# Two-layer hybrid decoder trunk: first unit of each layer and of an output projection as eight half products, forms ahead of the weights' splits

## The chip, the cores and the metric

The kernel runs on one core of a Trainium2 chip. The metric is the device time of one execution in microseconds (us), given as the median of several runs. Engines are called by their short names: PE is TensorE (matrix products, transposes), DVE is VectorE, ACT is ScalarE, POOL is GpSimd, SP is SyncE (it starts most transfers).

## The reference

Two layers work on x of 512 tokens and 2048 channels, one sequence. Cut to what matters:

```python
def fox_branch(x, w_in, b_f, q_gain, k_gain, w_out):        # layer 1, 16 heads of 128
    q, k, v, gate, f_logit = split(x @ w_in)                # 2048 -> 4 * 2048 + 16
    q, k = rms_norm(heads(q), q_gain), rms_norm(heads(k), k_gain)
    c = cumsum(log_sigmoid(f_logit + b_f))                  # the forget gate, per head
    p = softmax(causal(q @ k.T * scale + c[:, None] - c[None, :]))
    return (p @ v * silu(gate)) @ w_out                     # 2048 -> 2048

def retention_branch(x, w_in, w_out):                       # layer 2, 8 heads, qk 256, v 512
    q, k, v, gate = split(x @ w_in)                         # 2048 -> 2 * 2048 + 2 * 4096
    o = retain(rotary(q), rotary(k), v)                     # chunks of 128 with decay
    return (group_norm_heads(o) * silu(gate)) @ w_out       # 4096 -> 2048

x = layer_norm(alpha * x + fox_branch(x, ...))
x = layer_norm(alpha * x + retention_branch(x, ...))
```

Everything is float32.

## The kernel before

**Products.** Each factor of a large product is split into a high and a low part (`split`, L251 to L256): ACT rounds it into `h` (L255), then DVE subtracts to get `l` (L256). `mm3` (L258 to L262) makes high x high, high x low and low x high, three matmuls for one product.

**Units.** The projections are cut into 34 units. A unit takes the 512 tokens by 2048 input channels of one activation times a piece of the weights: narrow units 512 output columns (16 of them: q and k of a pair of heads), wide ones 1024 (18: gate and value, and the output projections). A `Unit` is computed by a scheme with seven products of quarters. The activation is cut into a11, a12, a21, a22: first index the half of the tokens, second the half of the input channels. The products use *forms* of it (`FORM`, L38): p1 a11, p2 a12, p3 s4, p4 a22, p5 s1, p6 s2, p7 s3, where s1 = a21 - a22, s2 = s1 - a11, s4 = s2 + a12, s3 = a11 - a21 (signs as the kernel keeps them). Weight quarters are summed likewise on DVE (L447, L451) and then split. Each product is worked in *blocks*: 2 blocks of 24 matmuls with 256 columns in a narrow unit, 4 blocks of 12 matmuls with 512 columns in a wide one. Results gather in three banks of accumulators (b0 to b2), are kept in SBUF by ACT (L339), combined on DVE (L367, L372, L377) and given to a *sink*, which is what the unit is for: `Pair.take` (q, k), `gate_and_value`, `add_z` (residual sum and statistics for the layer norm).

**Forms.** A form is made once and used by many units. x's quarters come from memory (`form_of_x`, `quarter_of_x`), and `combine` (L530) makes s1, s2, s4, s3 and a22 from them, a sum and a split at a time. For an output projection the heads write their output, with signs, into DRAM tiles that add up to the forms (`give_forms`, L588), and `fetch_form` (L596) loads and splits them (`y_raw`). The last two heads of layer 1 skip DRAM: `last_heads` (L923) splits their part of every form from the head's own output. Between the layers `to_columns` (L1109) normalises, transposes on PE (L1162) and evicts with the norm's gain (L1150 on DVE, L1152 on ACT), from which forms are made again.

**The order.** It is fixed when the program is built, by the class `Order`. Each block is a slot. In `slot` (L158) the weights are loaded up to 9 blocks ahead, summed and split 2 to 3 blocks ahead (`split_one`), the block is multiplied, then other work (heads, sinks, forms) takes one step per task (`step`, L114), as long as the estimated queues of DVE and ACT stay below 5.0. Before a block is multiplied, `require(b.ready)` (L134) lets such steps go until its form is there; by then the weights of the next blocks have been split already.

**The sequence.** Layer 1: `begin` (L510) with the first q/k unit and the first gate/value unit, on a11 and a12 (p1, p2), then the REST of both; then units in turn, with heads spawned by `core`. A pair's q and k are squared and summed on ACT (L756), scaled, transposed (L780), split (L774, L775), and each head's scores, softmax and values follow (`head`, L785). Two wide units make the output projection: unit 4 in the order `HELD`, unit 5 in `EARLY`. Layer 2 starts with `begin` again, then heads 1 to 7, then units 14 to 17, of which the last is `EARLY` too and ends in `store` (L1423): norm factors on DVE, two DVE steps for 512 columns (L1432, L1433), transfers to the output.

```python
BEGIN = (("p1",), ("p2",))
HELD = ([("p1", c) for c in range(4)] + [(p, c) for p in ("p5", "p6", "p2") for c in range(3)]
        + [(p, 3) for p in ("p5", "p6")] + blocks_of(4, ("p3", "p7")) + [("p2", 3)] + blocks_of(4, ("p4",)))
EARLY = (("p1", "p5"), ("p2", "p6"), ("p3",), ("p7",), ("p4",))
```

Of the kernel before, what the change touches and what calls it, by code (L numbers as in the profile page):

```python
# [17 lines left out]
P = 128  # L18
D = 2048
S = 512  # L20
# [19 lines left out]
        "s3": ("f10", "f11"), "a22": ("f12", "f13")}  # L40
# [3 lines left out]
def blocks_of(n, *groups):  # L44
# [4 lines left out]
BEGIN = (("p1",), ("p2",))  # L49
# [3 lines left out]
EARLY = (("p1", "p5"), ("p2", "p6"), ("p3",), ("p7",), ("p4",))  # L53

HELD = ([("p1", c) for c in range(4)] + [(p, c) for p in ("p5", "p6", "p2") for c in range(3)]
        + [(p, 3) for p in ("p5", "p6")] + blocks_of(4, ("p3", "p7")) + [("p2", 3)] + blocks_of(4, ("p4",)))
# [8 lines left out]
RINGS = dict(mmp=2, tmp=4, st=3, q=4, **{t: 1 for t in "k0 k1 k2 in0 in1 g0 g1 g2 d0 b0 b1 b2".split()})  # L65

# [9 lines left out]
class Order:  # L76
# [29 lines left out]
    def spawn(self, steps, front=False):  # L106
        task = dict(steps=steps, last=self.now - 1)
        try:
            task["need"] = next(steps)
        except StopIteration:  # L110
            return
        self.tasks.insert(0, task) if front else self.tasks.append(task)

    def step(self, forced=False):  # L114
        for task in list(self.tasks):
            n = task["need"]
            if self.now < task["last"] + n.get("wait", 1) or not n.get("until", lambda: True)():
                continue
# [3 lines left out]
            if not forced and any(d + c > 5.0 and c for d, c in zip(self.debt, cost)):  # L122
                continue
            self.debt = [d + c for d, c in zip(self.debt, cost)]
            self.time += n.get("pe", 0)
            task["last"] = self.now
            try:
                task["need"] = next(task["steps"])
            except StopIteration:
                self.tasks.remove(task)  # L130

    time = 0.0

    def require(self, met):  # L134
        for _ in range(400):
            if met():
                return
            self.turn()
            self.debt = [max(0.0, d - 2.7) for d in self.debt]
            self.step(True)  # L140
# [44 lines left out]
    def split_one(self):  # L185
        self.line[self.split].split()
        self.split += 1
        self.debt[0] += 1.22
        self.debt[1] += 1.06
# [7 lines left out]
def trunk(ctx: ExitStack, tc: tile.TileContext, xq, x, fb_f, columns, wf_in, narrow, wide, ln_g, ln_b, rot, decay,  # L197
# [80 lines left out]
    class Unit:  # L278
# [3 lines left out]
        def __init__(self, w, n, sink, rows=True, u2="k0"):  # L282
# [4 lines left out]
            self.tags = self.both = None  # L287
            self.early = False
            self.bank, self.kept, self.chain, self.lent, self.summed = {}, {}, {}, {}, {}
            self.left = {p: self.blocks for p in FORM}  # L290

# [3 lines left out]
        def accumulator(self, b):  # L295
            if self.both is None:
                if self.tags is None:
                    self.tags = dict(zip("xzy", banks))
                    banks[:] = banks[1:] + banks[:1]
                require(lambda: free[self.tags[b]])  # L300
                take(self.tags[b])
                t = psum.tile([P, 2, 512], F32, name="acc", tag=self.tags[b])
                return t if self.wide else t[:, 0].rearrange("p (e n) -> p e n", e=2)
            if b == "z":
                require(lambda: free[self.third])
                take(self.third)
                t = psum.tile([P, 2, 512], F32, name="acc", tag=self.third)[:, 0]
            else:
                if b == "x":
                    require(lambda: free[self.both])  # L310
                    take(self.both)
                    self.pair = psum.tile([P, 2, 512], F32, name="acc", tag=self.both)
                t = self.pair[:, int(b == "y")]
            return t.rearrange("p (e n) -> p e n", e=2)

        def leave(self, b):

            if self.both is None:
                give(self.tags[b])
            elif b != "y":  # L320
                give({"x": self.both, "z": self.third}[b])
# [32 lines left out]
        def after(self, p):  # L354
# [21 lines left out]
            if p == "p7":  # L376
                nc.vector.tensor_sub(k["p5"][0], k["p5"][0], b["x"])  # L377
                o.debt[0] += cost
                self.hand(1, 1, "p5")
            if p == "p4" and not self.early:  # L380
                self.sink(1, 0, b["x"], lambda after=0: self.leave("x"))
            if p == "p4" and self.early:
# [1111 lines left out]
```

## Time and profile before

| | |
|---|---|
| median of 3 runs | 2819.68 us (2817.28 to 2823.34) |
| the profiled execution: its time | 2814.23 us |
| its span in the trace | 2812.5 us |
| granted PE clock, mean | 0.931 of full |
| instructions | 34239 |
| moved by DMA | 488.98 MB, 174 GB/s |

The span is the time from the first to the last record of the profiled execution; all times inside it are counted from its start. Busy times of engines overlap. PEclk is the clock that PE was granted, as a share of full speed. In the rows of a timeline stand start, duration, engine, line, operation, output <- inputs, shape, and in brackets how long the engine had been idle before and what it then got.

### The profile page before, as it was taken

To read this page: it belongs to the slowest core of one execution; us is meant where nothing else is said; L and a number is where in the kernel's file an instruction comes from. 1 tells how busy PE (TensorE), PEld (TensorE's weight loads), DVE (VectorE), ACT (ScalarE), POOL (GpSimd) and SP (SyncE) were. 2 spreads that over 40 slices of the span, in tenths; PEclk is the share of its full clock that TensorE was granted. 3 is DMA by queue.
4 is the path that set the end of the run, shared out by engine and by line. 5 is a ranking of instruction groups with operands and counts; after the bars stand their busy time and mean duration, and the time that the engine had idled before them with its cause. 6 is when DMAs were issued, how large, how long until landed. Compare 5 with 4: busy or idle time off the path is not lost. (4 is left out here: it accounts for less than half of the span.)

```text
span 2812.5 us, 34239 instructions
## 1 busy us (share of the span) xinstructions
PE 2421.5 (86%) x12820; PEld 2044.4 (73%) x12820; DVE 2015.2 (72%) x2584; ACT 1280.6 (46%) x1898; POOL 190.8 (7%) x284
## 2 busy tenths in 40 slices
PE   6589989989997668875899999999999999699965
PEld 5478778788787447654687979797979787577754
DVE  5467767767766437754687888888888888677858
ACT  4244655655655533352344454545444445444422
POOL 0000100100100100100001010101010000010000
PEclk9699999999998679986999999999999999899987
DMA  5344654644645327632456575756575757587773
GB/s 204 105 151 145 184 164 147 199 149 143 187 150 172 103 86 230 210 127 69 145 186 191 180 211 168 201 161 195 176 213 170 212 159 235 149 252 245 228 230 118
DMA packets 195638, 488.98 MB, mean 174 GB/s; under 512 B 19264, under 2 KB 70080, under 8 KB 195216
## 3 DMA queue, kind: packets, MB, share of 16 engines
q1 hardware_dynamic: 165904, 415.74, 44.5%
q0 software_dynamic: 29568, 71.06, 11.0%
q8 instruction: 101, 1.65, 0.2%
q14 instruction: 65, 0.53, 0.1%
HBM read 419.84 MB, written 66.88 MB: 173 GB/s over the span
## 5 line engine op out<-in xcount | busy, mean ns | idle before, releaser
L255 ACT ACTIVATE w_h<-w_q 128x1024 fp32r<-128x1024 f32 x408 | 429.9, 1058 | 770.4 <-DVE w_q L451 531.9
L256 DVE TENSOR_TENSOR w_l<-w_q,w_h 128x1024 fp32r<-128x1024 f32 x408 | 497.9, 1223 | 334.7 <-ACT w_h L255 331.5
L260 PE MATMUL acc<-w_h,s 128*128 128x512 f32 (+1 forms) x1664 | 619.9, 373 | 98.3 <-ACT s L255 60.8
L261 PE MATMUL acc<-w_l,s 128*128 128x512 f32 (+1 forms) x1664 | 618.2, 372 | 34.2 <-DVE w_l L256 34.0
L262 PE MATMUL acc<-w_h,s 128*128 128x512 f32 (+1 forms) x1664 | 609.7, 366 | 9.5 <-DVE s L256 9.4
L256 DVE TENSOR_TENSOR w_l<-w_raw,w_h 128x1024 fp32r<-128x1024 f32 x312 | 380.3, 1223 | 255.0 <-ACT w_h L255 253.1
L260 PE MATMUL acc<-w_h,a 128*128 128x512 f32 (+1 forms) x1248 | 466.8, 374 | 63.4 <-ACT w_h L255 21.2
L255 ACT ACTIVATE w_h<-w_raw 128x1024 fp32r<-128x1024 f32 x312 | 326.3, 1054 | 372.2 <-DVE w_raw L447 192.9
L262 PE MATMUL acc<-w_h,a 128*128 128x512 f32 (+1 forms) x1248 | 459.9, 369 | 5.0 <-DVE a L256 5.0
L261 PE MATMUL acc<-w_l,a 128*128 128x512 f32 (+1 forms) x1248 | 460.2, 369 | 2.3 <-DVE w_l L256 2.3
L260 PEld LDWEIGHTS acc<-w_h,s 128*128 128x128 f32 x1664 | 326.3, 196 | 159.2 <-ACT s L255 65.3
L261 PEld LDWEIGHTS acc<-w_l,s 128*128 128x128 f32 x1664 | 325.9, 196 | 106.6 <-DVE w_l L256 63.5
L451 DVE TENSOR_TENSOR w_q<-w_q,w_raw 128x1024 f32<-128x1024 f32 x304 | 371.2, 1221 | 26.1 <-DMA w_raw<-in_wide 23.1
L262 PEld LDWEIGHTS acc<-w_h,s 128*128 128x128 f32 x1664 | 325.0, 195 | 58.4 <-DVE s L256 14.2
L260 PEld LDWEIGHTS acc<-w_h,a 128*128 128x128 f32 x1248 | 247.0, 198 | 103.8 <-issue 25.4
L262 PEld LDWEIGHTS acc<-w_h,a 128*128 128x128 f32 x1248 | 246.1, 197 | 44.7 <-DVE a L256 8.3
L261 PEld LDWEIGHTS acc<-w_l,a 128*128 128x128 f32 x1248 | 247.1, 198 | 38.4 <-DVE w_l L256 4.3
L260 PE MATMUL acc<-s,w_h 128*128 128x256 f32 x512 | 151.2, 295 | 31.5 <-ACT s L255 31.5
L261 PE MATMUL acc<-s,w_h 128*128 128x256 f32 x512 | 151.4, 296 | 7.4 <-DVE s L256 7.4
L262 PE MATMUL acc<-s,w_l 128*128 128x256 f32 x512 | 150.0, 293 | 0.0
L447 DVE TENSOR_TENSOR w_raw<-w_raw 128x1024 f32<-128x1024 f32 x96 | 117.0, 1219 | 23.9 <-DMA w_raw<-in_wide 23.9
L260 PEld LDWEIGHTS acc<-s,w_h 128*128 128x128 f32 x512 | 103.8, 203 | 34.2 <-ACT s L255 33.0
(206 smaller groups left out, 2956.2 us busy)
## 6 DMA issues: line engine op xcount, KB each, us to landing
w_raw<-in_wide SPq DMA_DIRECT2D x372, 512.0 KB, 3.6
w_raw<-in_narrow SPq DMA_DIRECT2D x164, 512.0 KB, 3.4
w_q<-in_wide SPq DMA_DIRECT2D x72, 512.0 KB, 4.2
w_q<-in_narrow SPq DMA_DIRECT2D x32, 512.0 KB, 4.4
y_s<-ny POOLq DMA_DIRECT2D x48, 256.0 KB, 6.9
y_s<-y POOLq DMA_DIRECT2D x40, 256.0 KB, 4.9
y_raw<-y_s SPq DMA_DIRECT2D x35, 256.0 KB, 4.9
y_raw<-y_a SPq DMA_DIRECT2D x26, 256.0 KB, 5.1
```

What stands on the lines that cost most here:

```text
L255: nc.scalar.activation(h, src, AF.Copy)
L256: nc.vector.tensor_sub(l, src, f32(h))
L260: nc.tensor.matmul(ps, a[0], b[0], start=start, stop=False, skip_group_check=True)
L261: nc.tensor.matmul(ps, a[0], b[1], start=False, stop=False, skip_group_check=True)
L262: nc.tensor.matmul(ps, a[1], b[0], start=False, stop=stop, skip_group_check=True)
L447: nc.vector.tensor_add(self.t, self.t, u.lent.pop(("p3", c)))
L451: nc.vector.tensor_add(u.chain[c], u.chain[c], t)
```

## The change

1. **Eight half products.** The first q/k unit of layer 1, the first q/k unit of layer 2 and the first unit of layer 1's output projection become units of a new class `Plain`. It computes C11 = a11 B1 + a12 B2 and so on directly: for both halves m of the tokens, both halves n of the output columns and both halves k of the input, the block (k, n, c, m) multiplies a form a(m)(k) by a weight block as it is. No weights are summed, a split weight block serves m = 0 and m = 1, and only the forms a11, a12, a21, a22 are used (a21 is a new form, at s3's place in SBUF). The orders are `BOTH` (layer 1), `EACH` (layer 2: first m = 0, then two products of the gate/value unit, then m = 1) and a new `HELD`. `begin`, `last_heads` and their parts go; heads 14 and 15 split only their a12 and a22.
2. **Order.** `split_one` first lets the form that a block needs go ahead of that block's weights' split. Tasks have ranks: sinks 0, forms and norms 1, heads 2; `step` goes on until no task goes any further. Limits are 4.8 (DVE) and 4.0 (ACT). A head's steps are cut finer.
3. **Smaller parts.** The squares for the norm of q and k are made by the sink, in place on the finished accumulator (L860 after), and `rsqrt` works in place; one more step stands between transposes and scores. `EARLY` makes p1, then p5; p7 and p4 are added to the residual in two parts, and the very last product in two halves. `store` works on one block of 128 tokens at a time, and half of the output transfers start on POOL's queue.

```diff
+BOTH = [(k, n, c, m) for k in (1, 2) for c in range(2) for n in range(2) for m in range(2)]
+EACH = [[(k, n, c, m) for k in (1, 2) for c in range(2) for n in range(2)] for m in range(2)]
-HELD = ([("p1", c) for c in range(4)] + [(p, c) for p in ("p5", "p6", "p2") for c in range(3)]
-        + [(p, 3) for p in ("p5", "p6")] + blocks_of(4, ("p3", "p7")) + [("p2", 3)] + blocks_of(4, ("p4",)))
+HELD = ([(1, 0, c, m) for c in range(4) for m in range(2)] + [(1, 1, c, 0) for c in range(4)]
+        + [(2, 0, c, m) for c in range(4) for m in range(2)] + [(1, 1, c, 1) for c in range(4)]
+        + [(2, 1, c, m) for c in range(4) for m in range(2)])
...
+    def step(self, forced=False, rank=2):
+
+        went = False
+        while self.each(forced, rank):
+            went = True
+        return went
...
     def split_one(self):
-        self.line[self.split].split()
+        b = self.line[self.split]
+        if b.before:
+            b.before()
+
+        self.require(b.ready)
+        if b.split():
+            self.debt[0] += 1.22
+            self.debt[1] += 1.06
         self.split += 1
-        self.debt[0] += 1.22
-        self.debt[1] += 1.06
...
+    class PlainBlock:
...
+        def split(self):
+            if self.same:
+                self.w = self.same.w
+                return False
+            self.w = [pool.tile(self.u.shape, F32R, name=f"w_{j}", tag=f"w_{j}", bufs=3) for j in "hl"]
+            split(self.t, *self.w)
+            give("st")
+            return True
+
+        def ready(self):
+            n = self.u.shape[1]
+            return ready.get(f"a{self.m + 1}{self.k}", set()).issuperset(range(n * self.c, n * self.c + n))
...
-            for s in range(ST):
-                yield need(act=2.0, mmp=1)
-                sq = by4(mmp())
-                for h in range(4):
-                    nc.scalar.activation(sq[:, h], raw[s][:, h * P:(h + 1) * P], AF.Square,
-                                         accum_out=ss[:, s, h:h + 1])
-                give("mmp")
...
-                yield from last_heads(head - 8, y)
-                give("tmp")
-                return
+
+                yield need(dve=0.8, act=0.8, until=lambda: len(ready["a12"]) >= 6 and len(ready["a22"]) >= 6)
+                for m in range(2):
+                    split_form(f"a{m + 1}2", y[:, None, m * 256:(m + 1) * 256], head - 8, head - 7)
...
-    Unit(wide, 4, sink).run(HELD, then={"p6": lambda s=steps: spawn(s())})
+    Plain(wide, 4, sink, last_banks).run(
+        HELD, then={8: lambda s=steps: spawn(s(), 1), 20: fetch("s1", "s2", "s4", "s3")})
...
-    begin(heads[0].qk_unit, heads[0].vg_unit, True)
-    for h in heads:
-        order = ORDER if h.h else REST
-        h.qk_unit.run(order, then={"p3": lambda h=h: spawn(h.attend())})
+    first.qk_unit.run(EACH[0], then={0: lambda: spawn(combine(True, first.qk_unit), 1)})
+    first.vg_unit.run(FIRST)
+    first.qk_unit.run(EACH[1], then={len(EACH[1]) - 1: lambda: spawn(first.attend())})
+    first.vg_unit.run(REST, then={"p4": lambda: spawn(first.retain())})
```

How this moves instructions is shown at three places. First DVE in the first two units, from the point where x's forms are split. Names are output <- inputs; `w_l` is the low part of a weight block, made from a loaded `w_raw` or a summed `w_q`; L545 is the sum for s1. Before:

```order
L256 TENSOR_TENSOR a12_176<-raw_145,a12_175 128x1024 x2
L256 TENSOR_TENSOR w_l_184<-w_raw_164,w_h_183 128x1024
L256 TENSOR_TENSOR w_l_217<-w_raw_173,w_h_216 128x1024
L256 TENSOR_TENSOR w_l_250<-w_raw_187,w_h_249 128x1024
L256 TENSOR_TENSOR w_l_281<-w_raw_189,w_h_280 128x1024
L367 TENSOR_TENSOR p15_246<-acc_191,p15_246 128x512
L256 TENSOR_TENSOR w_l_313<-w_raw_220,w_h_312 128x1024
L256 TENSOR_TENSOR w_l_336<-w_raw_253,w_h_335 128x1024
L256 TENSOR_TENSOR w_l_354<-w_raw_284,w_h_353 128x1024
```

And now the start of DVE's program:

```order
L282 TENSOR_TENSOR a11_153<-raw_143,a11_152 128x512 x2
L282 TENSOR_TENSOR w_l_159<-w_raw_149,w_h_158 128x1024
L282 TENSOR_TENSOR a21_165<-raw_145,a21_164 128x1024
L282 TENSOR_TENSOR w_l_169<-w_raw_162,w_h_168 128x1024
L282 TENSOR_TENSOR a11_153<-raw_143,a11_152 128x1024
L282 TENSOR_TENSOR w_l_236<-w_raw_173,w_h_235 128x1024
L282 TENSOR_TENSOR a21_165<-raw_145,a21_164 128x1024
L282 TENSOR_TENSOR w_l_292<-w_raw_176,w_h_291 128x1024
L282 TENSOR_TENSOR a12_348<-raw_144,a12_347 128x1024
L282 TENSOR_TENSOR w_l_352<-w_raw_179,w_h_351 128x1024
L282 TENSOR_TENSOR a22_382<-raw_146,a22_381 128x1024
L664 TENSOR_TENSOR raw_206<-raw_145,raw_146 128x1024
```

One form piece now stands ahead of each weight split, and the first sum for s1 (L664, L545 before) is the 12th row of the program instead of the 18th.

Second, ACT at the last two heads of layer 1: `o` is a head's output, `y_raw` a piece of a form loaded from DRAM, `y_s` a sum made in `last_heads`, `w_h` the high part of a weight block. Before, for the two heads:

```order
L255 ACTIVATE a12_7729<-y_raw_8409 128x512
L255 ACTIVATE w_h_8438<-w_raw_8352 128x1024
L255 ACTIVATE s4_7630<-y_raw_8453 128x512
L255 ACTIVATE a22_7806<-y_raw_8457 128x512
L255 ACTIVATE a12_7729<-o_8314 128x256
L255 ACTIVATE a22_7806<-o_8314 128x256
L255 ACTIVATE s1_7938<-y_s_8451 128x256
L255 ACTIVATE s2_7497<-y_s_8451 128x256
L255 ACTIVATE s4_7630<-y_s_8451 128x256
L897 ACTIVATE o_8474<-mmp_8445 128x512
L255 ACTIVATE a12_7729<-o_8474 128x256
```

Now:

```order
L281 ACTIVATE a12_7739<-o_8360 128x256
L281 ACTIVATE a22_7836<-o_8360 128x256
L922 ACTIVATE pT_8368<-mmp_8372 128x3x128
L1020 ACTIVATE ny_8389<-o_8360 128x512
L922 ACTIVATE pT_8368<-mmp_8383 128x2x128
L922 ACTIVATE pT_8368<-mmp_8383 128x128
L1004 ACTIVATE o_8402<-mmp_8397 128x512
L281 ACTIVATE a12_7739<-o_8402 128x256
L281 ACTIVATE a22_7836<-o_8402 128x256
L281 ACTIVATE w_h_8414<-w_raw_8005 128x1024
```

The s forms of these heads have gone from here, the loaded pieces stand further ahead, and the weights' split comes behind the forms.

Third, DVE where the second half of the tokens comes out of the layer norm's transposes at the start of layer 2 (`raw` is evicted, L1150 before, L1229 now). Before:

```order
L1150 TENSOR_SCALAR raw_9711<-mmp_9831,cols_75 128x128
L1150 TENSOR_SCALAR raw_9711<-mmp_9848,cols_75 128x128
L1150 TENSOR_SCALAR raw_9710<-mmp_9857,cols_75 128x128
L1150 TENSOR_SCALAR raw_9710<-mmp_9866,cols_75 128x128
L1150 TENSOR_SCALAR raw_9711<-mmp_9875,cols_75 128x128
L1150 TENSOR_SCALAR raw_9711<-mmp_9884,cols_75 128x128
L545 TENSOR_TENSOR raw_9896<-raw_9710,raw_9711 128x1024
L256 TENSOR_TENSOR s1_9898<-raw_9896,s1_9897 128x1024
```

Now:

```order
L1229 TENSOR_SCALAR raw_9688<-mmp_9744,cols_75 128x128
L282 TENSOR_TENSOR a21_9775<-raw_9688,a21_9774 128x1024
L282 TENSOR_TENSOR w_l_9779<-w_raw_9602,w_h_9778 128x1024
L1229 TENSOR_SCALAR raw_9689<-mmp_9769,cols_75 128x128
L282 TENSOR_TENSOR w_l_9806<-w_raw_9632,w_h_9805 128x1024
L1229 TENSOR_SCALAR raw_9689<-mmp_9800,cols_75 128x128
L282 TENSOR_TENSOR w_l_9835<-w_raw_9662,w_h_9834 128x1024
L1229 TENSOR_SCALAR raw_9688<-mmp_9827,cols_75 128x128
```

The evictions stand one by one between the weights' splits of blocks that use a11 and a12, and a21 is split as soon as its half is there; s1's sum stands 15 rows below the last one shown.

591 lines of the change are left out of this document (322 added, 269 removed).

## The prediction

> **What bounds the kernel now.** The page came first: its busy line and two rows of its table of slices, which share the span into 40 (digits are tenths).
>
> ```profile
> PE 2421.5 (86%) x12820; PEld 2044.4 (73%) x12820; DVE 2015.2 (72%) x2584; ACT 1280.6 (46%) x1898; POOL 190.8 (7%) x284
> ...
> PE   6589989989997668875899999999999999699965
> ...
> PEclk9699999999998679986999999999999999899987
> ```
>
> TensorE is the bound wherever its digit is 9, so only the dips can give much: the first slices, those from the 13th to the 20th, and the end. Next I read busy time by stage, cutting where one stage's last matmul or transpose hands over to the next.
>
> ```profile
> core 0: us, PE busy (x) PEld busy (x) DVE busy (x) ACT busy (x) POOL busy (x), PEclk, DMA share, GB/s
> 0.00:219.40 219.40, 154.78 (x769) 132.64 (x770) 121.20 (x122) 79.25 (x111) 2.87 (x11) 0.84 0.43 150
> 219.40:890.70 671.30, 619.12 (x3873) 548.11 (x3872) 473.73 (x699) 378.99 (x754) 62.74 (x93) 0.97 0.53 166
> 890.70:1187.00 296.30, 217.64 (x847) 166.97 (x845) 172.94 (x267) 128.20 (x227) 18.34 (x24) 0.81 0.52 161
> 1187.00:1426.70 239.70, 164.22 (x752) 135.45 (x753) 136.88 (x161) 84.92 (x116) 2.14 (x4) 0.80 0.34 113
> 1426.70:2350.00 923.30, 892.68 (x5033) 765.85 (x5032) 764.37 (x944) 432.42 (x509) 78.60 (x114) 1.00 0.63 188
> 2350.00:2812.50 462.50, 373.09 (x1554) 295.38 (x1552) 346.06 (x395) 176.78 (x183) 26.07 (x38) 0.92 0.66 207
> ```
>
> The stages are: **A**, the first two units; **F**, the rest of the forgetting layer's input; **O**, its output projection; **R**, the first two units of the retention layer; **S**, its other heads; **T**, the end. A, O and R hold 755 us, 219 of them without a running matmul, and much of the rest at a clock of 0.80 to 0.84. S has clock 1.00 and 3% idle. What TensorE waits for is told by its waits (us in all, times, longest) and by single rows of the timeline (start, duration, idle before in brackets).
>
> ```profile
> PE acc L260 <- ACT s L255: 92.3, 18, 12.6
> ```
> ```profile
> 8.84 0.58 PE L260 MATMUL acc<-w_h,a 128*128 128x256 f32 x1 [8.84 <-ACT w_h L255]
> 49.63 0.36 PE L260 MATMUL acc<-w_h,s 128*128 128x256 f32 x1 [3.76 <-ACT w_h L255]
> 59.39 0.58 PE L260 MATMUL acc<-w_h,s 128*128 128x256 f32 x1 [5.28 <-ACT s L255]
> 205.83 0.77 PE L260 MATMUL acc<-w_h,a 128*128 128x512 f32 x1 [6.58 <-ACT w_h L255]
> 906.57 0.80 PE L260 MATMUL mmp<-qk_h 128*128 128x512 f32 x1 [6.11 <-ACT qk_h L774]
> 975.17 0.79 PE L260 MATMUL mmp<-qk_h 128*128 128x512 f32 x1 [2.97 <-ACT qk_h L774]
> 997.25 2.32 PE L891 MATMUL mmp<-pT,by_head 128*128 128x512 f32 x8
> 1021.26 0.80 PE L260 MATMUL acc<-w_h,a 128*128 128x512 f32 x1 [6.75 <-ACT a L255]
> 1042.12 0.79 PE L260 MATMUL acc<-w_h,s 128*128 128x512 f32 x1 [12.56 <-ACT s L255]
> 1187.14 0.82 PE L1162 MATMUL mmp<-ident,z 128*128 128x128 f32 x4 [4.91 <-DVE raw L1150]
> 1310.39 0.58 PE L260 MATMUL acc<-s,w_h 128*128 128x256 f32 x1 [9.65 <-ACT s L255]
> ```
>
> The longest wait, for the s forms, is where a layer begins and where the last heads' output has to become forms (the waits at 59, at 1042, at 1310). Each starts a slow stretch as well: the matmul behind it lasts 0.58 or 0.79.
>
> **The change, part by part.** Unit costs first: back-to-back matmuls at full and at half clock.
>
> ```profile
> 10.69 0.41 PE L260 MATMUL acc<-w_h,a 128*128 128x256 f32 x1
> 13.04 0.41 PE L262 MATMUL acc<-w_h,a 128*128 128x256 f32 x1
> 13.64 0.28 PE L260 MATMUL acc<-w_h,a 128*128 128x256 f32 x1
> 14.71 0.28 PE L260 MATMUL acc<-w_h,a 128*128 128x256 f32 x1
> 2779.32 0.39 PE L260 MATMUL acc<-w_h,a 128*128 128x512 f32 x1
> 2782.50 0.39 PE L262 MATMUL acc<-w_h,a 128*128 128x512 f32 x1
> ```
>
> From 13.64 to 14.71 are 9 steps: 0.12 us for 256 columns; from 10.69 to 13.04 are 11: 0.21. From 2779.32 to 2782.50 are 14: 0.227 for 512. A narrow block of 24 costs 2.88 us, a wide one of 12 costs 2.73. Eight half products in place of seven add 2 narrow blocks to each of two units and 4 wide ones to one: 4 x 2.88 + 4 x 2.73 = 22.4 us more TensorE work, counted below.
>
> *A.* The first unit no longer needs a single s form: 16 blocks, 46.1 us, on plain quarters of x, while the vector engine makes s1 behind them. The second unit has 28 blocks, 76.4. The forget gate has 96 matmuls of 256 columns, 11.5. Start 8.8 plus 2 at half clock. Waits: one form now stands ahead of each weight split in both engines' queues, so that the weights' high and low parts queue behind it; I take 13 us (the 6.6 at 205.83 stays; the forget gate's weights are queued behind s4 and s3, about 4; 2 for single blocks). Sum 158 against 219.4: a gain of 61, less 3 for the first heads' scores, which now begin in this stage: **58**; 45 if all the waits of this kind are twice as long, 65 without them.
>
> Here the clock matters. The wait of 3.76 us at 49.63 left it up (0.36 behind it), that of 5.28 at 59.39 dropped it (0.58). So I charge half clock to waits over 5 us alone. The Trainium skill (TensorE: Matmul & The Clock Gate, "The HAM clock gate") has an idle window of about 3.4 us after which the rate is halved. By it each of some seven remaining waits of 3 to 5 us would cost 2 us more, 7 to 14 in all; the row at 49.63 speaks against it, one case only.
>
> *F.* Nothing is left out here; the order is finer. Idle time is 52 us, from which a gain can come, and the trace has waits like this one.
>
> ```profile
> 359.58 0.50 PE L260 MATMUL mmp<-qk_h 128*128 128x512 f32 x1 [3.35 <-ACT qk_h L774]
> ```
> ```profile
> L756 ACT ACTIVATE mmp<-qk_raw 128x128 f32<-128x128 f32 x128 | 35.7, 279 | 12.4 <-DVE o L904 4.7 <-DVE sm L849 4.6
> ```
>
> The added step between transposes and scores lets a block cover such a wait: 3.35 in each of some four pairs, about 13. The squares for the norms move onto the finished accumulator, which comes free later (16 squares a pair of 0.28, 4.5 us): some is lost again. The lower limits on what a slot may add to either engine's queue spread the heads' steps, at no cost I can see while TensorE is busy 92% here. Taken as a gain of **10**; bounds are a loss of 20 (six pairs with one more wait of 3.35) and a gain of 45 (nearly all idle time).
>
> *O.* Before, the s forms of the last two heads end the chain, at 1042.12, 151 us into the stage, and their loads hold up ScalarE's queue, and TensorE's behind it.
>
> ```profile
> 1035.33 0.63 ACT L255 ACTIVATE s<-y_raw 128x512 fp32r<-128x512 f32 x1 [7.48 <-DMA y_raw<-y_s]
> ```
>
> Now only a12 and a22 are needed, the last two heads' straight from their output, and no product of the unit waits for s1, s2 or s4; 18 of the 32 blocks stand ahead of head 15. Head 14 went from its scores at 975.17, 84 into the stage, to its product with the values at 997.25 in 22. With hardly a block between the last heads' steps in the new order, head 15 follows close: I take forms complete at 110 (84 + 22 and a few), between 95, if the scores come earlier too, and 131, where the wait for the forms of heads 12 and 13 ended (1021.26). Then follow 14 blocks and a second unit of 28, whose s forms are fetched from block 20 on, 12 blocks (33 us) ahead: 42 x 2.73 = 114.7, plus 12 for waits (before, 43 blocks, 117.4, took 145 from 1042 to 1187, 27 over; about half stays, the vector engine's sums of weights and of z). 110 + 115 + 12 = 237: gain **60**, between 25 (131 and 27) and 80.
>
> *R.* Again 16 narrow blocks, 46.1, and 28 wide, 76.4; transposes with their evictions about 12; the start's waits for a11 (4.9 in the row at 1187.14, the like for a12) and later ones, 20 together. That is 155, and 5 for scores that the first head now does after the next unit has begun: 160 against 239.7, gain **80**, 60 to 95. What hides the s forms' work now is 68 us of plain blocks; if that cover fails, the 9.65 of 1310.39 is paid again per form.
>
> *S, T.* Late in S nothing changes. At the end the norm's factors are taken for four token blocks apart.
>
> ```profile
> 2768.84 0.38 DVE L1101 BATCH_NORM_AGGREGATE ln_mv<-ln_st 128x2 f32<-128x24 f32 x2
> 2771.64 0.16 DVE L251 SCALAR_TENSOR_TENSOR ln_r<-rsq_t,ln_r 128x2 f32<-128x2 f32 x1
> 2782.50 0.39 PE L262 MATMUL acc<-w_h,a 128*128 128x512 f32 x1
> 2808.45 0.75 DVE L1433 SCALAR_TENSOR_TENSOR z<-z,ln_r,ln_last 128x512 f32<-128x512 f32 x1
> ```
>
> One chain takes 3 us; two more, 6, on the engine that works alone for 26 us after the last matmul. Halving p4 and starting blocks earlier gives some of that back: a loss of **3**, between 8 lost and 4 won. The outputs on the other queue have nobody behind them.
>
> Sum: 58 + 10 + 60 + 80 - 3 = 205. The profiled execution took 2814.2, so 2609; the runs' median is 5.5 above it: **2615**.
>
> **Rivals.** *The chains hold (0.20).* In O and R the heads' and the norm's serial steps, not the s forms, end the stage, and plain blocks only fill the wait and add work. For it: from 906.57 to 997.25, 91 us of stage O, the heads' steps hold no s form. Then O gains 20, R 40: 58 + 10 + 20 + 40 - 3 = 125, or 2695. *The finer steps clear the loop (0.12).* F gains its 45 instead of 10: 2580. *Forms block the weights (0.04), the slower side.* Both engines run in order, so a form's split ahead of the weights' waits for its load and holds them up.
>
> ```profile
> y_raw<-y_s SPq DMA_DIRECT2D x35, 256.0 KB, 4.9
> ```
> ```profile
> L255 ACT ACTIVATE s<-y_raw 128x1024 fp32r<-128x1024 f32 (+1 forms) x24 | 23.9, 997 | 19.7 <-DMA y_raw<-y_s 19.7
> L255 ACT ACTIVATE a<-y_raw 128x1024 fp32r<-128x1024 f32 (+1 forms) x18 | 18.1, 1004 | 15.2 <-DMA y_raw<-y_a 15.1
> ```
>
> With 42 such splits, a whole landing of 4.9 each and 2.2 of slow clock behind it, 300 us, 2915; it turns slower from 29 of the 42 on. Against it: the wait is 0.8 on average, and two split blocks, 5.5 us, are in hand. *Extra work eats the gain (0.01):* no change. The order shows that the change does what it says.
>
> **How the numbers follow.** The likeliest case has 0.63, and of itself reaches from 2560 to 2665 (the terms' ends added as squares: 13, 30, 30, 20, 6 give 50). The range takes in most of the other two: 2560 to 2700. Faster by over 0.2% (what a measurement here can tell from none): 0.63 + 0.20 + 0.12 = 0.95; the same 0.01; slower 0.04.
>
> **What would show it.** Right: no wait for an s form over 5 us near the start and behind the first layer; the second unit beginning near 70; the first layer's output stage near 237 and the retention start near 160, clocks above 0.9. Wrong: O above 265 with scores or a12 as the wait (the chains); F longer than 690; waits of an engine for a loaded form in S or T.

## The result and the profile after

The changed kernel takes 2693.49 us (median of 4 runs, 2688.65 to 2697.62), the kernel before 2818.48 in the same comparison: ratio 0.9554, 95% interval 0.9533 to 0.9574. That is 125 us faster, where the prediction's likeliest case said 205 (2615) and its range ended at 2700. Direction and range held. The size did not, and, as the experiments show, neither did the reason: that the time lies inside the range, 6 us from its end, owes much to luck.

The profiled execution has a span of 2686.9. From its page, busy time and two rows of slices:

```profile
PE 2395.3 (89%) x12964; PEld 2022.5 (75%) x12964; DVE 1964.9 (73%) x2551; ACT 1256.2 (47%) x1879; POOL 212.4 (8%) x316
...
PE   8889998998999697887889999999999998799975
...
PEclk9999999999999798999999999999999999899987
```

The dips have narrowed, and 144 more matmuls are busy for 26 us less, since fewer run at half clock (the mean granted clock is 0.961, before 0.931). Next comes busy time by stage, with the columns of the prediction's table and its cuts for A, F, O and R. Its stages S and T are divided anew into head 1, heads 2 to 6, and the rest:

```profile
0.00:175.40 175.40, 146.33 (x833) 124.80 (x834) 107.51 (x116) 75.51 (x112) 2.85 (x11) 0.95 0.45 158
175.40:839.00 663.60, 611.76 (x3873) 541.77 (x3872) 473.49 (x697) 377.45 (x769) 72.98 (x109) 0.99 0.55 169
839.00:1092.40 253.40, 209.39 (x856) 162.76 (x854) 134.94 (x218) 109.76 (x190) 25.36 (x32) 0.89 0.60 180
1092.40:1270.30 177.90, 147.06 (x801) 124.56 (x802) 125.71 (x145) 87.08 (x116) 2.13 (x4) 0.93 0.45 152
1270.30:1430.90 160.60, 142.16 (x767) 120.70 (x766) 122.61 (x153) 66.63 (x80) 11.83 (x18) 0.96 0.54 168
1430.90:2118.30 687.40, 665.22 (x3712) 567.00 (x3711) 567.47 (x697) 316.69 (x376) 57.00 (x83) 1.00 0.61 187
2118.30:2686.90 568.60, 473.38 (x2133) 380.90 (x2131) 433.15 (x529) 223.13 (x241) 40.23 (x59) 0.93 0.65 202
```

The kernel before, with the same division of its last part:

```profile
1426.70:1565.30 138.60, 133.48 (x743) 114.82 (x742) 113.94 (x142) 64.58 (x76) 12.00 (x19) 0.99 0.63 191
1565.30:2247.80 682.50, 662.01 (x3711) 567.26 (x3710) 567.51 (x697) 320.36 (x376) 56.78 (x83) 1.00 0.63 189
2247.80:2812.50 564.70, 470.27 (x2133) 379.14 (x2132) 428.98 (x502) 224.25 (x240) 35.88 (x51) 0.93 0.65 202
```

| stage | before | after | gain | forecast |
|---|---|---|---|---|
| A, first two units | 219.4 | 175.4 | 44 | 58 |
| F, rest of layer 1's input | 671.3 | 663.6 | 8 | 10 |
| O, its output projection | 296.3 | 253.4 | 43 | 60 |
| R, first two units of layer 2 | 239.7 | 177.9 | 62 | 80 |
| head 1 | 138.6 | 160.6 | -22 | 0 |
| heads 2 to 6 | 682.5 | 687.4 | -5 | 0 |
| rest | 564.7 | 568.6 | -4 | -3 |

Three of TensorE's waits in the changed kernel (us in all, times, longest):

```profile
PE acc L286 <- ACT w_h L281: 71.1, 19, 18.3
PE acc L287 <- DVE w_l L282: 40.9, 76, 1.3
...
PE acc L286 <- ACT qk_raw L1298: 10.4, 1, 10.4
```

The s forms, 92 us before, are gone from the list. What is waited for most now is the weights: `w_h` is a block's high part (47 us before) and `w_l` its low part (36 before).

### The profile page after: what moved, and what is told of

The parts are those of the page before. It is cut to its first block, busy times and chain, and to the rows that moved or that the text cites. A ratio compares the mean times of both kernels' runs of the same rounds, so it can differ in the third digit from the quotient of the medians.

```text
span 2686.9 us, 34465 instructions
## 1 busy us (share of the span) xinstructions
PE 2395.3 (89%) x12964; PEld 2022.5 (75%) x12964; DVE 1964.9 (73%) x2551; ACT 1256.2 (47%) x1879; POOL 212.4 (8%) x316
## 4 chain that ended last, share of the span: by engine, by line
PE 26%; DVE 21%; ACT 7%; DMA 6%; issue 5%; SPq 0%; ACTq 0%; DVEq 0%
PE acc L287 8%; PE acc L286 8%; PE acc L288 8%; DVE w_l L282 7%; ACT w_h L281 5%; DVE w_q L470 5%; DMA w_raw<-in_wide 4%; DMA y_raw<-y_a 1%; DVE w_raw L466 1%; PE mmp L287 1%; PE mmp L288 1%; PE mmp L286 1%; DMA y_raw<-y_s 1%; DVE rope L1323 1%; DVE s L282 1%
## 5 line engine op out<-in xcount | busy, mean ns | idle before, releaser
L281 ACT ACTIVATE w_h<-w_q 128x1024 fp32r<-128x1024 f32 x384 | 403.4, 1058 | 665.3 <-DVE w_q L470 507.2
L282 DVE TENSOR_TENSOR w_l<-w_q,w_h 128x1024 fp32r<-128x1024 f32 x384 | 469.2, 1223 | 272.6 <-ACT w_h L281 269.9
L286 PE MATMUL acc<-w_h,s 128*128 128x512 f32 (+1 forms) x1536 | 575.9, 375 | 71.5 <-ACT w_h L281 48.6
L287 PE MATMUL acc<-w_l,s 128*128 128x512 f32 (+1 forms) x1536 | 576.5, 375 | 37.7 <-DVE w_l L282 37.3
L288 PE MATMUL acc<-w_h,s 128*128 128x512 f32 (+1 forms) x1536 | 564.2, 367 | 0.0
L286 PE MATMUL acc<-w_h,a 128*128 128x512 f32 (+1 forms) x1408 | 511.2, 363 | 37.3 <-ACT w_h L281 22.4
L282 DVE TENSOR_TENSOR w_l<-w_raw,w_h 128x1024 fp32r<-128x1024 f32 x324 | 394.4, 1223 | 203.1 <-ACT w_h L281 201.8
L287 PE MATMUL acc<-w_l,a 128*128 128x512 f32 (+1 forms) x1408 | 507.0, 360 | 3.6 <-DVE w_l L282 3.6
L281 ACT ACTIVATE w_h<-w_raw 128x1024 fp32r<-128x1024 f32 x324 | 339.3, 1054 | 358.2 <-DVE w_raw L466 183.2
L288 PE MATMUL acc<-w_h,a 128*128 128x512 f32 (+1 forms) x1408 | 505.3, 359 | 0.0
L286 PEld LDWEIGHTS acc<-w_h,s 128*128 128x128 f32 x1536 | 298.2, 194 | 129.6 <-ACT w_h L281 55.5
L470 DVE TENSOR_TENSOR w_q<-w_q,w_raw 128x1024 f32<-128x1024 f32 x280 | 341.7, 1220 | 35.2 <-DMA w_raw<-in_wide 32.4
L288 PEld LDWEIGHTS acc<-w_h,s 128*128 128x128 f32 x1536 | 298.0, 194 | 43.1
L286 PEld LDWEIGHTS acc<-w_h,a 128*128 128x128 f32 x1408 | 270.8, 192 | 77.5 <-ACT w_h L281 24.0
L288 PEld LDWEIGHTS acc<-w_h,a 128*128 128x128 f32 x1408 | 270.1, 192 | 38.3 <-DVE a L282 0.2
L286 PE MATMUL acc<-a,w_h 128*128 128x256 f32 x464 | 133.1, 287 | 10.6 <-ACT qk_raw L1298 10.4
L288 PE MATMUL acc<-a,w_l 128*128 128x256 f32 x464 | 132.3, 285 | 1.2 <-DVE w_l L282 1.2
L287 PE MATMUL acc<-a,w_h 128*128 128x256 f32 x464 | 132.1, 285 | 0.0
L286 PE MATMUL acc<-s,w_h 128*128 128x256 f32 x448 | 127.4, 284 | 3.1 <-ACT p L351 3.1
```

The source lines that it names most:

```text
L281: nc.scalar.activation(h, src, AF.Copy)
L282: nc.vector.tensor_sub(l, src, f32(h))
L286: nc.tensor.matmul(ps, a[0], b[0], start=start, stop=False, skip_group_check=True)
L287: nc.tensor.matmul(ps, a[0], b[1], start=False, stop=False, skip_group_check=True)
L288: nc.tensor.matmul(ps, a[1], b[0], start=False, stop=stop, skip_group_check=True)
L470: nc.vector.tensor_add(u.chain[c], u.chain[c], t)
```

## The experiments

The main table comes first, with stages in us of one profiled execution each and medians of the timed runs. The letters are those above, h1 is head 1, h2-6 heads 2 to 6. Heads' work moves over the cuts from kernel to kernel (O has 847 matmuls before, 856 after and 794 in e3), so a single stage compares to some us only.

| kernel | A | F | O | R | h1 | h2-6 | rest | median | ratio to before (95%) |
|---|---|---|---|---|---|---|---|---|---|
| before | 219.4 | 671.3 | 296.3 | 239.7 | 138.6 | 682.5 | 564.7 | 2818 | 1 |
| after | 175.4 | 663.6 | 253.4 | 177.9 | 160.6 | 687.4 | 568.6 | 2693 | 0.9554 (0.9533-0.9574) |
| e2, after, weights first | 189.8 | 667.4 | 263.5 | 195.4 | 163.9 | 689.5 | 576.1 | 2747 | 0.9750 (0.9734-0.9766) |
| e3, before, forms ahead | 179.0 | 688.2 | 249.3 | 193.7 | 143.7 | 684.2 | 570.9 | 2712 | 0.9626 (0.9611-0.9640) |
| e1, after, sums ahead | 167.7 | 646.3 | 247.3 | 171.3 | 153.8 | 670.5 | 552.2 | 2613 | 0.9275 (0.9261-0.9289) |
| e6, before, sums ahead | 211.6 | 649.3 | 290.6 | 228.8 | 132.0 | 659.3 | 549.3 | 2727 | 0.9675 (0.9660-0.9691) |
| e5, before, both orders | 173.0 | 672.6 | 239.0 | 183.2 | 131.6 | 659.4 | 553.9 | 2621 | 0.9300 (0.9282-0.9317) |
| e10, see below | 153.3 | 651.9 | 260.9 | 181.6 | 135.5 | 667.9 | 551.8 | 2603 | 0.9239 (0.9221-0.9257) |
| e12, see below | 155.0 | 645.6 | 254.3 | 184.8 | 134.2 | 660.7 | 552.5 | 2589 | 0.9183 (0.9171-0.9196) |

### Which half of the change carries the gain

The prediction put nearly all of the gain down to the half products, which need no s form. Two kernels take one half each. In e2 the changed kernel loses the order:

```diff
     def split_one(self):
         b = self.line[self.split]
         if b.before:
             b.before()
 
-        self.require(b.ready)
         if b.split():
```

> The changed kernel with one half of the change taken back: the weights' split no longer waits for the form of its block, so weights go ahead of forms in both engines' order again; half products and all else stay. If the half products carry the gain: 2693 to 2705. If the order carries it: 2733 or more, with s forms among the longest waits again. If forms ahead of weights cost time (they put evictions and splits between the two engines' steps): below 2688.

It took 2747, slower than the changed kernel by 54. The second case holds, and s forms are back among TensorE's waits:

```profile
PE acc L285 <- ACT s L280: 34.7, 9, 8.9
```

In e3 the kernel before gets the order and nothing else:

```diff
     def split_one(self):
-        self.line[self.split].split()
+        b = self.line[self.split]
+        if b.before:
+            b.before()
+        self.require(b.ready)
+        b.split()
         self.split += 1
...
-            if self.before:
-                self.before()
```

> The kernel before, with one half of the change alone: a block's form goes ahead of that block's weights' split; no half products, no new ranks, old limits. If the half products carry the gain: 2800 to 2825 (before 2818). If the order carries it: 2780 or less, the 92 us of waits for s forms more than halved. Slower than 2825 if forms that wait for loads hold up the weights.

It took 2712. A few lines in `split_one`, without a single half product, bring 104 to 106 of the 125 us. Without them, all the rest of the change brings 69 to 71 (e2); on top of them it brings some 20. Both do the same job, which is to get rid of the waits for s forms, and so they don't add up. In e3 the first rows of TensorE's waits are:

```profile
PE acc L264 <- ACT w_h L259: 79.7, 19, 17.8
PE acc L265 <- DVE w_l L260: 44.4, 68, 3.6
PE acc L264 <- DVE p L381: 28.5, 13, 8.0
```

No s form is in the whole list, although all seven products are there. Why the order does it can be seen in the kernel before, ahead of the wait that ended at 98.63 (rows of VectorE and ScalarE, and the matmul that waited):

```profile
83.01 1.22 DVE L256 TENSOR_TENSOR s<-raw,s 128x1024 fp32r<-128x1024 f32 x1 [1.12 <-ACT s L255]
89.01 0.60 ACT L339 ACTIVATE u<-acc 128x512 f32<-128x512 f32 x1 [6.04 <-PE acc L262]
89.51 1.05 ACT L255 ACTIVATE w_h<-w_raw 128x1024 fp32r<-128x1024 f32 x1
90.59 1.23 DVE L256 TENSOR_TENSOR w_l<-w_raw,w_h 128x1024 fp32r<-128x1024 f32 x1 [6.35 <-ACT w_h L255]
91.73 1.22 DVE L447 TENSOR_TENSOR w_raw<-w_raw 128x1024 f32<-128x1024 f32 x1
92.86 2.36 DVE L557 TENSOR_TENSOR raw<-raw 128x1024 f32<-128x1024 f32 x2
95.13 1.22 DVE L560 TENSOR_TENSOR raw<-raw 128x1024 f32<-128x1024 f32 x1
96.27 1.22 DVE L562 TENSOR_TENSOR raw<-raw 128x1024 f32<-128x1024 f32 x1
97.53 1.06 ACT L255 ACTIVATE s<-raw 128x1024 fp32r<-128x1024 f32 x1 [6.97 <-DVE raw L562]
98.63 0.58 PE L260 MATMUL acc<-w_h,s 128*128 128x256 f32 x1 [9.66 <-ACT s L255]
```

From 84 to 90.6 VectorE stands idle with the sums for the next forms (L557 to L562) still to come in its program. Ahead of them is the low part of a weight block (90.59), which waits for its high part (89.51), and that stands in ScalarE's program behind the copy of a product that TensorE was still working on (89.01). So the form that TensorE needed next was begun only when TensorE had run dry, though both engines had had 6 us of idle time before. Neither engine was short of time here; the order was wrong. In e3 the same sums run ahead of a low part:

```profile
64.33 2.35 DVE L559 TENSOR_TENSOR raw<-raw 128x1024 f32<-128x1024 f32 x2
...
70.08 1.22 DVE L260 TENSOR_TENSOR s<-raw,s 128x1024 fp32r<-128x1024 f32 x1 [1.12 <-ACT s L259]
71.22 1.22 DVE L260 TENSOR_TENSOR w_l<-w_raw,w_h 128x1024 fp32r<-128x1024 f32 x1
```

### What the order left: sums, high and low parts in series

The changed kernel's second unit of layer 2 (20 blocks from 1194.5 to 1270.3) took 75.8 us, where 20 x 2.73 is 55. Its rows, sum (L470), high part (L281 on ACT) and low part (L282):

```profile
1206.06 1.22 DVE L470 TENSOR_TENSOR w_q<-w_q,w_raw 128x1024 f32<-128x1024 f32 x1
1207.39 1.06 ACT L281 ACTIVATE w_h<-w_q 128x1024 fp32r<-128x1024 f32 x1 [2.51 <-DVE w_q L470]
1208.48 1.23 DVE L282 TENSOR_TENSOR w_l<-w_q,w_h 128x1024 fp32r<-128x1024 f32 x1 [1.21 <-ACT w_h L281]
1209.62 1.22 DVE L470 TENSOR_TENSOR w_q<-w_q,w_raw 128x1024 f32<-128x1024 f32 x1
...
1213.17 1.22 DVE L470 TENSOR_TENSOR w_q<-w_q,w_raw 128x1024 f32<-128x1024 f32 x1
```

A sum begins every 3.56 us: at 1206.06, 1209.62, 1213.17. Since the next sum stands behind this block's low part, the three steps run one after the other over two engines, and a summed block costs 3.56, not 2.73. TensorE shows it only as short waits:

```profile
1209.76 0.50 PE L287 MATMUL acc<-w_l,s 128*128 128x512 f32 x1 [0.53 <-DVE w_l L282]
1213.31 0.51 PE L287 MATMUL acc<-w_l,s 128*128 128x512 f32 x1 [0.50 <-DVE w_l L282]
```

In e1 the next block's sum goes ahead of this block's low part:

```diff
-            while self.split < self.added:
-                self.split_one()
-            self.debt[0] += self.line[self.added].add()
+            b = self.line[self.added]
+            if any(x.u is b.u and x.c == b.c for x in self.line[self.split:self.added]):
+                while self.split < self.added:
+                    self.split_one()
+            self.debt[0] += b.add()
             self.added += 1
+            while self.split < self.added - 1:
+                self.split_one()
```

> The changed kernel, but on VectorE the sum of a block's weights goes ahead of the low part of the block before it (not where the two share weights). Chain theory: what the forecast left out is that summed blocks in a row run sum (1.22), high part on ScalarE (1.06), low part (1.23) one behind the other, 3.5 us a block, where TensorE needs 2.73. Then 0.8 us comes back for each of 12 such blocks in each layer's second unit and some 6 in the first layer's second output unit and in the last unit: 36 x 0.8 = 29 us, so 2664 (2650 to 2676) where the changed kernel takes 2693; the 20 blocks between 1194 and 1270 in 62 us in place of 76. Rival, VectorE is simply full in these stages (80% of 1194 to 1270): order makes no difference, 2693 within 5.

It took 2613, 80 less and far more than the 29 expected. The mechanism is right, since in the same place low parts and sums now follow one another without a gap:

```profile
1171.61 1.22 DVE L286 TENSOR_TENSOR w_l<-w_q,w_h 128x1024 fp32r<-128x1024 f32 x1
1172.74 1.22 DVE L474 TENSOR_TENSOR w_q<-w_q,w_raw 128x1024 f32<-128x1024 f32 x1
1173.88 1.22 DVE L286 TENSOR_TENSOR w_l<-w_q,w_h 128x1024 fp32r<-128x1024 f32 x1
1175.02 1.22 DVE L474 TENSOR_TENSOR w_q<-w_q,w_raw 128x1024 f32<-128x1024 f32 x1
```

Every 2.28 us a block could be ready, less than TensorE needs. The expected size was too small because I counted the slow stages and the last unit alone. By stage, F, heads 2 to 6 and the rest gained 16 to 17 us each, where TensorE was taken to be the bound. In A, O and R the gain was 6 to 8 each, so only a part of what those stages lack. The second unit of layer 2 went from 75.8 to 68.9 (1163.7 to 1232.6), not to 62.

e6 makes the same edit in the kernel before, without forms ahead:

> The kernel before with sums ahead of the low part of the block before, nothing else. Chain theory as a cost of its own, apart from the forms: it gains where summed blocks follow one another with no wait for forms, some 17 us each in the loop of layer 1, in heads 2 to 7 of layer 2 and at the end, and little in the three slow stages: 2816 to 2765 (2750 to 2780). Rival, the chain is also what makes the forms late: 2740 or less. Rival, it only matters once the forms are early: over 2800.

It took 2727, 92 less, and the loop of layer 1 (F), heads 2 to 6 and the rest gained 22, 23 and 15. The slow stages gained 8, 6 and 11. This agrees with a cost of its own, which is larger than expected; the rival bound of 2740 was passed as well, but not by way of the forms, whose waits stay (92.3 in the kernel before):

```profile
PE acc L264 <- ACT s L259: 94.2, 18, 12.7
```

e5 is the kernel before with both orders, e3's and e6's edits together:

> The kernel before with two changes of order and nothing else: forms ahead of the weights' splits, and sums ahead of the low part of the block before. No half products. If the order is all there is: 2712 (forms ahead alone) less the 80 that sums ahead brought in the changed kernel, 2632 (2620 to 2645), and the first two units, the first output projection and the first two units of layer 2 within 8 us each of the changed kernel with sums ahead. If half products are worth more once VectorE's chain no longer limits them: over 2655, with these stages 30 us longer together.

It took 2621. The ratios multiply: 0.9626 x 0.9675 = 0.9313, and 0.9300 was measured. The two orders are costs apart. And the whole of the change, half products, finer steps and all, with sums ahead (e1, 2613) is only 8 us better than the two orders alone, with intervals that overlap. In F it is 26 better; the finer steps may be the reason, but no run takes them back alone. Where half products act (A, O, R and head 1) e1 takes 740.1 and e5 726.8. Of the three stages that were to lie within 8 us of e1's, A does (5 longer), O hardly (8 shorter) and R does not (12 longer); head 1 is 22 shorter.

### The single terms

e4 took up the longest wait that was new, 10.4 us for a bank at the start of layer 2:

```profile
1169.80 0.58 PE L286 MATMUL acc<-a,w_h 128*128 128x256 f32 x1 [10.42 <-ACT qk_raw L1298]
```

```diff
-            self.vg_unit.tags = dict(x=a, y=b, z=b)
+            self.vg_unit.tags = dict(x=a, y=b, z=c)
+            self.qk_unit.tags = c, b
             banks[:] = c, b, a
-            return c, c
...
-    first.qk_unit.run(EACH[0], then={0: lambda: spawn(combine(True, first.qk_unit), 1)})
-    first.vg_unit.run(FIRST)
+    first.vg_unit.run(FIRST, then={0: lambda: spawn(combine(True, first.qk_unit), 1)})
+    first.qk_unit.run(EACH[0])
     first.qk_unit.run(EACH[1], then={len(EACH[1]) - 1: lambda: spawn(first.attend())})
```

> The changed kernel with another order at the start of layer 2: the two products of the gate and value unit that need a11 and a12 first, then both halves of q and k in two different banks. Bank theory: the wait of 10.4 us at 1169.8 is for the bank of the first half, which can't be drained while the norm's tiles hold its buffers; it goes, 2684 (2681 to 2688). Rival: the wait only changes its name, since a21 and a22 are split no earlier than 1169 anyway: 2691 to 2695.

It took 2698, ratio 0.9575 (0.9559 to 0.9590): no gain, 3 us over the rival's range. The wait went and another came in its place, in the norm's transposes:

```profile
1100.56 0.69 PE L1243 MATMUL mmp<-ident,z 128*128 128x128 f32 x2 [13.70 <-DVE raw L1231]
```

e7 takes the squares of q and k off the finished accumulator again:

```diff
-                yield need(act=2.0)
-                for e in range(2):
-                    for h in range(2):
-                        v = tile[:, e, h * P:(h + 1) * P]
-                        nc.scalar.activation(v, v, AF.Square, accum_out=self.ss[:, 2 * m + e, 2 * n + h:2 * n + h + 1])
...
+            for s in range(ST):
+                yield need(act=2.0, mmp=1)
+                sq = by4(mmp())
...
```

> The changed kernel with the squares of q and k taken again in the pair's own step, by way of a spare bank, and no more on the finished accumulator. Forecast: squares in place hold the accumulator and cost some 5 us of the loop's gain, so 2688 (2683 to 2692). If they are what makes the loop 25 us shorter than in the kernel before with forms ahead: 2710 or more. If neither: 2693 within 4.

It took 2682, ratio 0.9519 (0.9503 to 0.9535), 11 less, just below the forecast's 2683. The loop gained 8, near the 5 that this forecast had given to the squares in place; the greater part was elsewhere. Stage A fell by 15, to the 161 that the prediction has for it, and O grew by 8. Part of that is work that moved: A has 16 matmuls fewer than the changed kernel and is busy with them for 4.9 us less, O has 15 more:

```profile
0.00:160.50 160.50, 141.39 (x817) 121.76 (x818) 102.57 (x99) 73.07 (x104) 2.84 (x11) 0.98 0.50 172
160.50:816.20 655.70, 611.24 (x3874) 544.99 (x3872) 473.87 (x706) 380.42 (x752) 72.87 (x109) 0.98 0.55 171
816.20:1077.20 261.00, 210.98 (x871) 164.23 (x868) 138.46 (x227) 117.74 (x212) 25.36 (x32) 0.88 0.58 174
```

e8 takes the added step between transposes and scores away (one `yield need()`):

> The changed kernel without the added step between a pair's transposes and its scores. Forecast: the step lets a block cover waits of 3.35 us in four pairs, so 13 us are lost: 2706 (2700 to 2710). If the finer cut of the heads covers them anyway: 2693 within 4.

It took 2696, ratio 0.9562 (0.9542 to 0.9582): no effect. The step that the forecast gave 13 us covers nothing that the finer cut doesn't cover. e11 lets a task take only one step in a slot again:

```diff
-        while self.each(forced, rank):
-            went = True
+        went = self.each(forced, rank)
         return went
```

> The changed kernel, where a task takes one step in a slot again and not as many as go. If this, with the heads' finer cut, is what keeps the loop of layer 1 at 664 us where forms ahead alone made it 688: 2715 or more. If it doesn't matter: 2693 within 5.

It took 2800, ratio 0.9940 (0.9923 to 0.9957), which undoes nearly the whole gain. Only 12 of it are in the loop; the output projection takes 346 instead of 253:

```profile
851.90:1197.80 345.90, 249.91 (x959) 187.49 (x957) 148.20 (x261) 136.38 (x262) 39.29 (x50) 0.79 0.51 146
```

The heads' work lags behind the blocks, so that 103 more matmuls fall into this stage than in the changed kernel, and TensorE's waits for heads' steps there come to 58 us in place of 21. I read it so that a head cut into finer steps, one to a slot, becomes a chain that nothing covers. Finer steps and several to a slot belong together.

### Putting together what helped

e9 is the changed kernel with the edits of e1 and e7:

> The changed kernel with both edits that helped: sums ahead of the low part of the block before (2613 alone) and squares taken again in the pair's own step (11 less than the changed kernel alone). If the two costs are apart: 2602 (2598 to 2606). If squares in place only hurt while VectorE's chain delays everything: 2610 to 2616.

It took 2612, ratio 0.9267 (0.9246 to 0.9288): nothing beyond e1, the second case. In it A gains 13 over e1, O loses 12 and F 3. e10 is e9 with seven products for layer 2's first unit: `Plain` becomes `Unit`, its order is p1 and p2 behind those of the gate/value unit, then the rest, and accumulators are shared as the kernel before did it.

> The kernel of e9, with layer 2's first unit as seven products of forms again, in the order that the kernel before had there (gate and value on a11 and a12, then q and k on a11 and a12, then the rest), and no a21 form. If the eight half products are worth having there: 2608 or more. If, as the stages of e5 against e1 say, the order alone did the work and half products cost 5.8 us of matmuls and more around them: 2592 (2586 to 2598).

It took 2603, between the two cases: 8 less than e9, with intervals that overlap. The stages say where, with R and head 1 together 317.1 in place of 324.7. So half products there show no gain once the order is right, and by the stages cost about what their extra matmuls cost. For layer 1's two units with half products no run takes them back alone. e12 is e10 with the old limits of 5.0 (`LIMIT = 5.0, 5.0`):

> The kernel of e10 with the old limits of 5.0 on both engines' estimated queues in place of 4.8 and 4.0. Heads 2 to 6 of layer 2 take 668 us in e10 and 660 in e5, which has the old limits: if these are the reason, 2595 (2590 to 2599). If finer steps and ranks are, 2603 within 4; slower than 2608 if the lower limits help layer 1.

It took 2589, ratio 0.9183 (0.9171 to 0.9196): 14 less than e10, the fastest of all, 105 below the changed kernel and 229 below the one before. Heads 2 to 6 take 660.7, the 660 expected, and the loop and the output projection of layer 1 are 6 shorter each, which was not expected. The lower limits cost more than they gave.

## Why the prediction was right or wrong

**The direction and where.** The three slow stages did hold the gain, and the 92 us of waits for s forms went. That was right, and so was the sign for A: its second unit began at 61, forecast near 70. O near 237 and R near 160 were missed (253 and 178), and O's clock was 0.89, not above 0.9.

**The cause, wrong.** The prediction put the gain down to products that need no s form and priced forms ahead of weights as waits of 13 us in A and as a rival that makes it slower. e3 and e2 show the reverse: the order alone brings 104 us, and in the stages A, O and R, where the prediction counted on half products, it gains 40, 47 and 46 without a single one. What forms ahead cost was small beside it: in e3 the waits for `w_h` rose from 47 to 80 us, and F took 17 longer. That the direction came out right was therefore luck as to the cause, since the change held both halves. The failed step was the reading "the longest wait is for the s forms, so the forms must not be needed". The trace could have told why a form was late: the 6.35 us in front of `w_l` at 90.59 stood in it.

**A block at 2.73, wrong for summed blocks.** Every sum of the prediction used 2.73 for the wide unit. In a row, summed blocks took 3.56. It was worth 80 us in the changed kernel, over all stages. The kernel before paid as much (92, e6), so where the forecast started from the time before, it is no part of the gain that failed to come; A, O and R were added up from 2.73 a block, and there and in head 1 it is 27 of the 71 us by which these fell short (by e1).

**A: 44 for 58.** Without squares in place this stage is 15 shorter (e7), about a third of it with 16 matmuls that moved to later stages; the prediction had charged the squares to F alone and with less.

**O: 43 for 60.** The heads' part was right. The last head's two forms were split at 943.5, complete 106 us into the stage, forecast 110:

```profile
943.53 0.73 ACT L281 ACTIVATE a<-o 128x256 fp32r<-128x256 f32 x2 [0.76 <-DVE o L1011]
957.83 0.47 PE L286 MATMUL acc<-w_h,a 128*128 128x512 f32 x1 [4.41 <-DVE z L1158]
```

From there to the transposes it took 147, forecast 127. In that are a wait for a bank that holds the first quarter until its residual is added (4.4, not foreseen) and the second unit's summed blocks in a row: e1 cuts the stage by 6. The rest stays open.

**R and head 1: 40 for 80.** R itself came out at 178 against 160, of which 5 were for scores that fall into head 1. In it are the 10.4 us for a bank, which e4 could not turn into time, and the second unit's pace (7 of its 21 us over, by e1). Head 1 then took 22 more, not 5: 24 more matmuls fall into it (767 for 743), and TensorE's longest wait in it is for the first head's q and k (`qk_h`, 6.3). Why these came late is not shown; VectorE was busy for 123 of the 161 us. With seven products, the sums ahead and the squares back (e10) head 1 takes 135.5.

**F: 8 for 10,** but the two parts were wrong: the step is worth nothing in all (e8), the squares cost 8 (e7), and several steps a slot, which had no term, are worth 12 (e11). **Rest: -4 for -3,** right as a sum; no run takes its terms apart. Heads 2 to 6 lost 5 that the prediction had at nothing. The limits are the likely reason there: in e12 the old ones bring 7.

**The rival at 2695.** Its time was met within 2 us, but not its mechanism: it had O gain 20 by heads' chains that hold, and the heads' forms were early. A chain of heads' steps decides only where a task has one step a slot (e11).

**The clock.** I charged half clock for waits over 5 us alone, on the word of one row: a wait of 3.76 at 49.63, with 0.36 for the matmul behind it. That row was read too soon. The stretch behind it, and those before and behind the end of a wait of 3.24 in the changed kernel (from 2263.16 to 2266.40), have these granted clocks (the column ahead of the DMA share):

```profile
49.60:53.20 3.60, 3.57 (x21) 3.60 (x22) 2.31 (x2) 0.52 (x1) 0.00 (x0) 0.67 0.47 162
53.20:54.10 0.90, 0.90 (x5) 0.62 (x3) 0.00 (x0) 0.00 (x0) 0.00 (x0) 0.50 0.88 346
```
```profile
2262.00:2266.30 4.30, 1.17 (x6) 0.63 (x4) 1.00 (x2) 2.55 (x4) 0.00 (x0) 0.93 0.93 348
2266.30:2270.00 3.70, 2.94 (x6) 2.05 (x7) 3.67 (x4) 1.00 (x2) 0.00 (x0) 0.50 0.59 175
```

0.67 over 3.6 us means some 1.2 us at full clock and half from there. So the clock fell about 1 us after the wait of 3.76 had ended, and some 0.6 us before the wait of 3.24 did (0.93 over 4.3 us). In the changed kernel it fell during each of the nine waits of 3 to 5 us or within 2 us behind it. The Trainium skill (TensorE: Matmul & The Clock Gate, "The HAM clock gate") says that the window is about 3.4 us and runs freely, not reset by the kernel's start. A moment that varies fits that; that a wait of 3.24, shorter than the window, was enough is what this trace shows. It was not so each time: the wait of 3.35 that ended at 359.58 in the kernel before left the clock at 1.00 up to 363. All the same, the prediction should have charged waits of 3 to 5 us too, 7 to 14 us by its own estimate.

## What to carry to other kernels

Where an engine waits long for something small, look in the maker's queue at what stands ahead of it, and whether that in turn waits for the waiting engine. Mend the order before the algorithm. Price a block by the chain of steps that makes it ready, over all engines, and not by the consumer's rate alone. When a change has two halves, price and run each by itself: here either half alone gave more than half of what both gave.

## What had not been expected

A TensorE that reads as full can hide a stall of each block. In heads 2 to 6 the page of stages gave 665.2 us busy of 687.4 at a clock of 1.00, so only 3% idle. In e5, with both orders in the kernel before, the same matmuls (3712 and 3711 in the records) are busy for 652.3 of 659.4:

```profile
1399.40:2058.80 659.40, 652.25 (x3711) 569.74 (x3710) 566.80 (x697) 321.12 (x377) 56.73 (x83) 1.00 0.64 196
```

Of the 28 us between the two (some 7 of them by the limits, if e12 holds here), 13 had been counted as busy: after a short wait a matmul lasts 0.50, as at 1209.76, where one in a row lasts 0.39. What tells it is the spacing of the blocks, not the busy share.
